# A diffusion-transformer block on one core: instructions of the attention stage kept at the program's place on their engines, and a read of a score bank moved

## The chip, the cores and the metric

The kernel runs on one core of a Trainium2 chip. The time is device time in microseconds (us) of one execution. The core has a matrix engine, TensorE (PE in the profile; its weight loads are listed as PEld), and VectorE (DVE), ScalarE (ACT), GpSimd (POOL) and SyncE (SP, which here issues transfers only). Each engine takes its instructions in the order of its own queue; semaphores order them between engines. POOL's queue issues transfers too.

## The reference

One block over 1024 tokens of width 2048, with 256 context tokens, 8 attention heads with two score maps each, pooling, convolution, and 16 experts:

```python
hx = modulate(rmsnorm(x, norm1_g), ...)          # hc the same of the context
qx, kx, vx, px, bx, cx, ix = split_groups(hx @ w_in)
k_all, v_all = concat(kc, rope(kx)), concat(vc, vx)         # 1280 keys
s = einsum('bqhmd,bkhmd->bhmqk', rope(qx), k_all) * 64 ** -0.5   # m = 0, 1
a = softmax(s)
att = einsum('bhqk,bkhe->bqhe', a[:, :, 0] - lam * a[:, :, 1], v_all)
pool = ((window sums of px) / count - px) @ pool_w * pool_scale  # windows 2, 4, 8, 16
z = cx * ix
conv = bx * (z[t - 1] * conv_w[0] + z[t] * conv_w[1] + z[t + 1] * conv_w[2])
x = x + mod * (concat(rmsnorm(att), pool, conv) @ w_out)
x = x + mod * expert_choice_ffn(modulate(rmsnorm(x, norm2_g)))   # 128 tokens an expert
return rmsnorm(x, final_g)
```

## The kernel before

The program goes through modulation and normalisation, the projections, the attention, the output projection with the normalisation and router behind it, and the experts. The change is in the attention.

**Attention steps.** There are 64 steps: one of 8 heads, one block of 256 tokens (`b`), and one half of it of 128 rows (`qt`). `score(i)` makes 18 matmuls for step i. They fill one PSUM tile `sc` of 128 x 2560 f32, which is five banks of 512 columns: columns 0 to 1279 are the first map, 1280 to 2559 the second. Each map is cut into three column groups (`CH`) that don't cross a bank, with three products for each; `PAIRED` (L920) lays both maps' products side by side, one map's on the upper 64 rows of the PE array and the other's on the lower 64. The bank of columns 1024 to 1535 holds the end of the first map, which comes first in its order, and the start of the second, which comes last in its order. Between the two stands a small read on ACT, "turned" (L965), of two columns of that bank. Then for each map DVE takes the maximum (`nm`, L970) and ACT the exponential with its sum (`e`, L975).

`combine(i)` divides the two sums (the reciprocal of L982, then L983, L984) and subtracts the second map's exponentials from the first's (L987). `turn` transposes the result on PE (`trw`), ACT casts it (`wth`, L1000) and DVE takes the rest (`wtl`, L1001). `value` multiplies by V once per two steps (`av`).

**What runs beside them.** Between these operations filler matmuls of the projections and of the output projection run on PE (`gm`); their weights are split in two parts by ACT (L439) and POOL (L440). `next_block()` (L910) is called at the start of each step: it computes the block that the previous call loaded, and loads the next one. A block is a pooling block (bias on ACT, L861; sums on POOL, L864 to L872; a matmul) or a convolution block (first product on ACT, L896; L897, L898 and L900 on DVE, in four blocks L902 on POOL in place of L900; then a split by L500 on ACT and L502 on DVE). There are 16 of each. Their data come by SP from DRAM into two buffers (`pl_x`, and `cv_z` in the same ring).

**Loads.** `load_q`, `load_k` and `load_v` issue from POOL's queue. K and Q have two buffers each. The step's part of the loop, in the program's order, is:

```python
next_block()
...
if nn and steps[nn][2] == 0:
    load_q(*steps[nn][:2])      # nn = i + 3
if new2:                        # step nn begins another head
    load_k(visit[nn])
...
even=['C', 'S', 0.3, 'V', 0.35, 0.0, 'T0', 0.3, 'T1', 'T2', 0.05],
odd=['C', 'S', 0.25, 'T0', 0.4, 'T1', 0.2, 'T2', 0.15],
```

'C' is `combine(i + 1)`, 'S' is `score(i + 2)`, 'V' `value`, 'T0' to 'T2' `turn`, and a number a share of the filler.

**What sets the order.** The program is written in that order, but `TileContext(schedule_with_timeline_sim=True)` reorders each engine's queue by a simulated timeline, within the dependencies. An instruction can so stand on its engine's queue far ahead of its place in the program, or behind it. `tc.keep_in_program_order(ins)` ties an instruction behind the one that the program issued just before it on the same engine. It adds no wait on the chip; it holds that instruction from floating ahead of that one, and no other instruction.

Of the kernel before, what the change touches and what calls it, by code (L numbers as in the profile page):

```python
# [9 lines left out]
F32 = mybir.dt.float32  # L10
# [4 lines left out]
AF = mybir.ActivationFunctionType  # L15
# [5 lines left out]
P = 128  # L21
# [6 lines left out]
QB = 256  # L28
# [128 lines left out]
def nosync(tc, later, earlier):  # L157
    if earlier is not None:
        tc.add_manual_dep(later.ins, earlier.ins.name,
                          mybir.DependencyInfo(mybir.DependencyClass.NoSync, mybir.DependencyReason.DATA),  # L160
                          reason="accumulation groups of one bank in order")


def block_kernel(tc, I, out, dbg=None):
    nc = tc.nc
    pe, act, dve, gp, sp = nc.tensor, nc.scalar, nc.vector, nc.gpsimd, nc.sync
# [3 lines left out]
    def mm(o, l, r, start=True, stop=True):  # L170
        return pe.matmul(o, l, r, start=start, stop=stop, skip_group_check=True)  # L171

    dr = mk("dram", space=DRAM)
    kS = [dr.tile([P, 2, NKEY], F32R, name=f"kS{h}") for h in range(HEADS)]
    qS = [dr.tile([P, 2, SEQ], F32R, name=f"qS{h}") for h in range(HEADS)]
    vS = [dr.tile([P, 2, NKEY], F32R, name=f"vS{h}") for h in range(HEADS)]
# [42 lines left out]
    cw_col = colB[:, 37:49]  # L219
# [9 lines left out]
    bias_pg = lsm  # L229
# [6 lines left out]
    def tr_bank(name, pool=None):  # L236
        return (pool or ptr).tile([P, 512], F32, name=name, tag="tr")
# [5 lines left out]
    t = tr_bank("trv")  # L243
# [250 lines left out]
    def hl_store(src, n, scale, dst, pool, bufs, key=None, bias=None, tag="e_hl"):  # L494
        p = pool.tile([P, 2, 512], F32R, name=tag, tag=tag, bufs=bufs)
        if bias is not None:
            act.activation(p[:, 0, :n], src, AF.Identity, bias=bias)
            dve.scalar_tensor_tensor(p[:, 1, :n], src, bias, raw(p[:, 0, :n]), op0=ALU.add, op1=ALU.subtract)
        else:
            act.activation(p[:, 0, :n], src, AF.Copy, scale=scale)  # L500
            if isinstance(scale, float) and scale == 1.0:
                dve.tensor_tensor(p[:, 1, :n], src, raw(p[:, 0, :n]), op=ALU.subtract)  # L502
            else:
                dve.scalar_tensor_tensor(p[:, 1, :n], src, scale, raw(p[:, 0, :n]), op0=ALU.mult, op1=ALU.subtract)
        step = P // len(dst)
        for i, d in enumerate(dst):
            sp.dma_start(raw(d), raw(p[i * step:(i + 1) * step, :, :n]))
        written.add(key)
# [66 lines left out]
    def run_chunk(*args, beside=None):  # L575
        c = ChunkA(*args)
        for k in range(KT):
            if beside:
                next(beside, None)
            c.step(k)  # L580
        run_later()
        return c
# [67 lines left out]
    for h in range(HEADS):  # L650
        c = run_chunk(OFF_Q + h * P)
# [7 lines left out]
    for g in range(4):  # L659
        c = run_chunk(OFF_GC + g * P)  # L660
# [4 lines left out]
        c = run_chunk(OFF_X + g * P)  # L665
# [10 lines left out]
    t = tr_bank("trm")  # L676
# [13 lines left out]
    sc = psc.tile([P, 2 * NKEY], F32, name="sc")  # L690
# [6 lines left out]
    asm = mk("asm", bufs=2, side="right")  # L697
# [69 lines left out]
    def after(n, f, kind="b"):  # L767
        due.append((pos["tick"] + n, kind, f))
        due.sort(key=lambda d: d[0])
# [88 lines left out]
        return lambda: pool_block(g, b, x, cn, biased)  # L858

    def pool_block(g, b, x, cn, biased):  # L860
        act.activation(biased, biased, AF.Identity, bias=bias_pg[:, g:g + 1])  # L861
        w = POOL_WINDOWS[g]
        y = evB.tile([P, WP], F32, name="pl_y", tag="pl_y", bufs=3)
        gp.tensor_tensor(y[:, 1:WP], x[:, 0:WP - 1], x[:, 1:WP], op=ALU.add)  # L864
        lo, hi, sh = 1, WP, 1
        while 2 * sh < w:
            y2 = evB.tile([P, WP], F32, name="pl_y", tag="pl_y", bufs=3)
            gp.tensor_tensor(y2[:, lo + sh:hi - sh], y[:, lo:hi - 2 * sh], y[:, lo + 2 * sh:hi], op=ALU.add)
            lo, hi, sh, y = lo + sh, hi - sh, 2 * sh, y2
        m = y[:, HALO:HALO + QB]  # L870
        gp.tensor_tensor(m, m, cn, op=ALU.mult)
        gp.tensor_tensor(m, m, x[:, HALO:HALO + QB], op=ALU.subtract)  # L872

        def rest():
            t = tr_bank("trp")
            mm(t[:, 0:QB], pw[:, g], m)
            hl_store(t[:, 0:QB], QB, psc_col[:, g:g + 1], [mixP[b][:, :, g, :]], evb, T["mhl"], ("m", b, g), tag="m_hl")
        after(T["a_pool"], rest)
# [14 lines left out]

    def conv_block(g, b, z, gb):
        y = evB.tile([P, QB], F32, name="e_out", tag="e_out", bufs=T["eo"])
        act.activation(y, z[:, 0:QB], AF.Copy, scale=cw_col[:, g:g + 1])  # L896
        dve.scalar_tensor_tensor(y, z[:, 1:1 + QB], cw_col[:, 4 + g:5 + g], y, op0=ALU.mult, op1=ALU.add)  # L897
        dve.scalar_tensor_tensor(y, z[:, 2:2 + QB], cw_col[:, 8 + g:9 + g], y, op0=ALU.mult, op1=ALU.add)  # L898
        if b < 3:
            dve.scalar_tensor_tensor(y, gb, bias_pg[:, 4 + g:5 + g], y, op0=ALU.add, op1=ALU.mult)  # L900
        else:
            gp.tensor_tensor(y, y, gb, op=ALU.mult)  # L902
        hl_store(y, QB, 1.0, [mixP[b][:, :, 4 + g, :]], evb, T["mhl"], ("m", b, 4 + g), tag="m_hl")
# [29 lines left out]
    K_, V_, Q_, E_, W_ = {}, {}, {}, {}, {}  # L933

    def load_k(v):
        assert ("k", v[0]) in written
        K_[v] = ksp.tile([P, 2, NKEY], F32R, name="ks", tag="ks")
        gp.dma_start(K_[v], kS[v[0]])

    def load_v(v, l):  # L940
        assert ("v", v[0]) in written
        t = vsp.tile([P, NKEY // P, P], F32R, name="vh" if l == 0 else "vl", tag=f"v{l}", bufs=2 - l)
        gp.dma_start(t, vS[v[0]][:, l].rearrange("p (k e) -> p k e", e=P))
        V_[v, l] = t

    def load_q(h, b):
        assert b < 3 or ("q", h) in written
        q = qsp.tile([P, 2, QB], F32R, name="qs", tag="qs")
        gp.dma_start(q, qS[h][:, :, b * QB:(b + 1) * QB])
        Q_[h, b] = q  # L950

    last_stt = [None]
# [2 lines left out]
    def score(i):  # L955
        h, b, qt = steps[i]
        q = Q_[h, b]
        k = K_[visit[i]]
        for _, m, c, n in PAIRED:
            c0, c1 = CH[m][c]  # L960
            rows = slice(64 * m, 64 * m + 64)
            one = mm(sc[:, m * NKEY + c0:m * NKEY + c1], q[rows, n // 2, qt * P:(qt + 1) * P], k[rows, n % 2, c0:c1],
               start=(n == 0), stop=(n == 2))
            if (m, c, n) == (0, 0, 2):
                act.copy(asm.tile([P, 2], F32, name="turned", tag="turned"), sc[:, c0:c0 + 2])  # L965
        scored.append(one)
        for m in range(2):
            s = sc[:, m * NKEY:(m + 1) * NKEY]
            nm = asm.tile([P, 1], F32, name="nm", tag=f"nm{m}")
            r = dve.tensor_reduce(nm, s, axis=AX, op=ALU.max, negate=True)  # L970
            if T["nsy"]:
                nosync(tc, r, last_stt[0])
            e = ep.tile([P, NKEY], F32, name=f"e{m}", tag=f"e{m}", bufs=(LEAD + 1, 2)[m])
            ssum = s0C[:, b, h, qt:qt + 1] if m == 0 else asm.tile([P, 1], F32, name="s1", tag="s1")
            act.activation(e, s, AF.Exp, bias=nm, scale=1.0, accum_out=ssum)  # L975
            E_[i, m] = (e, ssum)

    def combine(i):
        h, b, qt = steps[i]
        (e0, s0), (e1, s1) = E_[i, 0], E_.pop((i, 1))  # L980
        cf = asm.tile([P, 1], F32, name="cf", tag="cf")
        dve.reciprocal(cf, s1)  # L982
        dve.tensor_scalar(cf, cf, s0, neglam, op0=ALU.mult, op1=ALU.mult)  # L983
        dve.tensor_scalar(cf, cf, 2.0 ** 100, -(2.0 ** 100), op0=ALU.min, op1=ALU.max)  # L984
        for lo, hi in ((0, T["csplit"]), (T["csplit"], NKEY)):
            if hi > lo:
                last_stt[0] = dve.scalar_tensor_tensor(e0[:, lo:hi], e1[:, lo:hi], cf, e0[:, lo:hi], op0=ALU.mult, op1=ALU.add)  # L987
# [184 lines left out]
    if True:  # L1172
# [3 lines left out]
        sp.dma_start(pw, I["pool_w"][0].rearrange("g c d -> c g d"))  # L1176
        fill(T["f1"] - T["f0"])
        load_k(visit[0])
        load_q(*steps[0][:2])
        load_v(visit[0], 0)  # L1180
        load_v(visit[0], 1)
        fill(FIRST - T["f1"])
        run_all()
# [9 lines left out]
        for i in range(NS):  # L1193
            h, b, qt = steps[i]
# [12 lines left out]
            if new2:  # L1207
                load_k(visit[nn])
# [255 lines left out]
    t = pl.tile([P, 512], F32, name="trk", tag="rl", bufs=1)  # L1464
# [4 lines left out]
    t = pl.tile([P, 512], F32, name="trk2", tag="tr", bufs=2)  # L1469
# [119 lines left out]
    for stage in plan:  # L1589
        kind, e = stage[:2]  # L1590
# [17 lines left out]
        for k in range(nk):  # L1608
# [6 lines left out]
            if k == nk - 1:  # L1615
# [5 lines left out]
                else:  # L1621
                    y, hsl = y_[e], slice(half * 1024, (half + 1) * 1024)
# [40 lines left out]
```

## Time and profile before

| what | value |
|---|---|
| time, median of 3 runs | 3346.76 us (3344.51 to 3351.8) |
| time of the profiled execution | 3349.19 us |
| its span, first to last instruction | 3347.4 us |
| PE, DVE, ACT, POOL busy | 3070.2, 2258.2, 1768.6, 879.7 us |
| mean granted TensorE clock | 0.968 |
| PE busy, 870 to 1520 us (attention steps with blocks) | 554.61 of 650 us |
| PE busy, 1600 to 1860 us (late attention steps) | 252.09 of 260 us |
| PE busy, 2100 to 3347 us (experts) | 1155.79 of 1247 us |

The profiled execution is one of its own; its rows add up to its own time, and the difference of 1.79 us between time and span lies around the first and the last instruction. Rows of a timeline give the start in us, the duration in us, the engine, the line, the operation, output and inputs, and in brackets the idle time of the engine ahead of it with what ended it.

### The profile page before, as it was taken

How to read it: one execution, taken by the hardware profiler on the slowest of the kernel's cores; microseconds unless marked ns; L12 is line 12 of the kernel's file. 1: busy time of each engine (PE TensorE's matmuls, PEld its weight loads, DVE VectorE, ACT ScalarE, POOL GpSimd, SP SyncE). 2: the span in 40 equal slices, each digit the busy share in tenths (PEclk: the TensorE clock that was granted, in tenths of full speed). 3: DMA queues.
4: the chain of work that ended last, by engine and by line, in shares of the span. 5: the costliest groups of instructions: out<-in, count | busy, mean ns of one | idle time of the engine just before them, and what ended most of it. 6: DMA issues, size and time to landing. Idle time of an engine off the chain costs nothing. (4 is left out here: it accounts for less than half of the span.)

```text
span 3347.4 us, 48671 instructions
## 1 busy us (share of the span) xinstructions
PE 3070.2 (92%) x18783; PEld 2627.1 (78%) x18783; DVE 2258.2 (67%) x2744; ACT 1768.6 (53%) x2555; POOL 879.7 (26%) x581
## 2 busy tenths in 40 slices
PE   7999999999979889878999989699999999999995
PEld 4689989888868778777989878588777777777774
DVE  5235765662257766676555579788888888888877
ACT  5213322362245556554444344577766677676665
POOL 1001100010245555544667676220000000000021
PEclk9999999999989999999999999799999999999998
DMA  9965877633466555547787876899999999999998
GB/s 313 288 211 191 279 282 247 225 123 92 122 186 176 157 156 160 172 137 223 242 266 245 301 251 214 346 335 384 380 371 369 359 369 372 363 377 368 355 331 311
DMA packets 501851, 891.24 MB, mean 266 GB/s; under 512 B 24913, under 2 KB 356258, under 8 KB 490738
## 3 DMA queue, kind: packets, MB, share of 16 engines
q1 hardware_dynamic: 476960, 788.27, 67.2%
q0 software_dynamic: 24560, 99.83, 9.6%
q8 instruction: 147, 2.41, 0.3%
q14 instruction: 86, 0.70, 0.1%
q10 hardware_dynamic: 98, 0.03, 0.0%
HBM read 797.80 MB, written 90.23 MB: 265 GB/s over the span
## 5 line engine op out<-in xcount | busy, mean ns | idle before, releaser
L1443 DVE TENSOR_TENSOR es_t<-er_t,es_t 128x1024 fp32r<-128x1024 f32 x764 | 888.5, 1220 | 99.9 <-ACT es_t L1439 98.3
L1439 ACT CAST es_t<-er_t 128x1024 fp32r<-128x1024 f32 x768 | 775.8, 1052 | 181.0 <-PE gu L171 99.1
L440 POOL TENSOR_TENSOR w_split<-w_raw,w_split 128x1024 fp32r<-128x1024 f32 x208 | 547.1, 2636 | 441.3 <-ACT w_split L439 417.3
L171 PE MATMUL g_x<-hxh,w_split 128*128 128x512 f32 (+3 forms) x2560 | 592.5, 341 | 1.1 <-DVE w_split L440 1.1
L439 ACT CAST w_split<-w_raw 128x1024 fp32r<-128x1024 f32 x288 | 301.7, 1049 | 450.0 <-PE g_x L171 136.1
L171 PEld LDWEIGHTS g_x<-hxh,w_split 128*128 128x128 f32 x2560 | 396.7, 189 | 52.4 <-issue 9.9
L171 PE MATMUL gm<-w_split,mxh 128*128 128x256 f32 x2048 | 387.7, 289 | 11.3 <-DVE oy L1135 4.3
L171 PEld LDWEIGHTS gm<-w_split,mxh 128*128 128x128 f32 x2048 | 324.8, 194 | 17.6 <-issue 8.1
L171 PE MATMUL g_x<-hxl,w_split 128*128 128x256 f32 (+1 forms) x1280 | 331.6, 339 | 0.0
L171 PE MATMUL gu<-es_t,xh 128*128 128x512 f32 x1024 | 291.4, 405 | 22.5 <-DVE es_t L1443 22.5
L171 PE MATMUL dn<-es_t,hh 128*128 128x512 f32 x1024 | 300.0, 404 | 10.3 <-DVE es_t L1443 6.4
L171 PE MATMUL gm<-w_split,mxl 128*128 128x256 f32 x1024 | 293.9, 287 | 1.9 <-DMA mxl<-mixP 1.1
L171 PE MATMUL gg<-es_t,xh 128*128 128x512 f32 x1024 | 290.3, 400 | 1.1 <-ACT xh L1509 1.1
L171 PE MATMUL gm<-hbh,w_split 128*128 128x256 f32 x1280 | 272.8, 299 | 16.2 <-ACT e_raw L513 13.1
L970 DVE TENSOR_REDUCE nm<-sc 128x1 f32<-128x1280 f32 x128 | 190.6, 1489 | 130.2 <-ACT e L975 79.1
L975 ACT ACTIVATE e<-sc,nm 128x1280 f32<-128x1280 f32 x128 | 170.2, 1330 | 161.8 <-DVE nm L970 161.2
L171 PEld LDWEIGHTS gu<-es_t,xh 128*128 128x128 f32 x1024 | 195.1, 192 | 74.2 <-DVE es_t L1443 27.8
L171 PEld LDWEIGHTS dn<-es_t,hh 128*128 128x128 f32 x1024 | 189.6, 190 | 62.4 <-DVE es_t L1443 15.9
L1499 POOL DMA_INDIRECT xg<-h2S,idxT x16 | 23.2, 1448 | 818.9 <-PE tre L1507 738.1
L171 PEld LDWEIGHTS gm<-hbh,w_split 128*128 128x128 f32 x1280 | 214.4, 197 | 27.4 <-ACT e_raw L513 16.0
L171 PEld LDWEIGHTS gg<-es_t,xh 128*128 128x128 f32 x1024 | 190.7, 189 | 47.2 <-DVE es_t L1443 2.2
L171 PEld LDWEIGHTS g_x<-hxl,w_split 128*128 128x128 f32 x1280 | 198.2, 189 | 23.8 <-issue 3.3
(301 smaller groups left out, 5131.1 us busy)
## 6 DMA issues: line engine op xcount, KB each, us to landing
er_t<-in_w_gate SPq DMA_DIRECT2D x128, 1024.0 KB, 8.3
er_t<-in_w_down SPq DMA_DIRECT2D x128, 1024.0 KB, 8.8
er_t<-in_w_up SPq DMA_DIRECT2D x122, 1024.0 KB, 13.0
ada_w<-in_w_ada SPq DMA_DIRECT2D x192, 512.0 KB, 5.6
w_raw<-in_w_in SPq DMA_DIRECT2D x160, 512.0 KB, 4.7
w_raw<-in_w_out SPq DMA_DIRECT2D x128, 512.0 KB, 5.7
ks<-kS POOLq DMA_DIRECT2D x16, 1280.0 KB, 8.3
vh<-vS POOLq DMA_DIRECT2D x16, 640.0 KB, 5.5
```

The costliest lines, as they stand in the source:

```text
L171: return pe.matmul(o, l, r, start=start, stop=stop, skip_group_check=True)
L439: act.copy(s[:, 0], r)
L440: lo_eng.tensor_tensor(s[:, 1], r, raw(s[:, 0]), op=ALU.subtract)
L970: r = dve.tensor_reduce(nm, s, axis=AX, op=ALU.max, negate=True)
L975: act.activation(e, s, AF.Exp, bias=nm, scale=1.0, accum_out=ssum)
L1439: c = act.copy(s[:, 0], r)
L1443: lo = (gp if on_gp else dve).tensor_tensor(s[:, 1], r, raw(s[:, 0]), op=ALU.subtract)
L1499: ins = gp.indirect_dma_start(out=xg, out_offset=None, in_=h2S, in_offset=bass.IndirectOffsetOnAxis(ap=idxT[:, e:e + 1], axis=0))
```

## The change

Six instructions are tied to the program's place on their engine: the pooling block's bias and the convolution's first product on ACT, the loads of K, V and Q on POOL's queue, and the reciprocal that begins the combination on DVE. The read of the shared bank is issued just before the second map's first product into that bank, which is the 15th of the 18 matmuls; before, it was issued behind the first map's last product into it, the 4th.

```diff
     def pool_block(g, b, x, cn, biased):
-        act.activation(biased, biased, AF.Identity, bias=bias_pg[:, g:g + 1])
+        tc.keep_in_program_order(act.activation(biased, biased, AF.Identity, bias=bias_pg[:, g:g + 1]))
...
     def conv_block(g, b, z, gb):
         y = evB.tile([P, QB], F32, name="e_out", tag="e_out", bufs=T["eo"])
-        act.activation(y, z[:, 0:QB], AF.Copy, scale=cw_col[:, g:g + 1])
+        tc.keep_in_program_order(act.activation(y, z[:, 0:QB], AF.Copy, scale=cw_col[:, g:g + 1]))
...
-        gp.dma_start(K_[v], kS[v[0]])
+        tc.keep_in_program_order(gp.dma_start(K_[v], kS[v[0]]))
...
-        gp.dma_start(t, vS[v[0]][:, l].rearrange("p (k e) -> p k e", e=P))
+        load = gp.dma_start(t, vS[v[0]][:, l].rearrange("p (k e) -> p k e", e=P))
+        tc.keep_in_program_order(load)
...
-        gp.dma_start(q, qS[h][:, :, b * QB:(b + 1) * QB])
+        tc.keep_in_program_order(gp.dma_start(q, qS[h][:, :, b * QB:(b + 1) * QB]))
...
         for _, m, c, n in PAIRED:
             c0, c1 = CH[m][c]
             rows = slice(64 * m, 64 * m + 64)
+            if (m, c, n) == (1, 2, 0):
+                act.copy(asm.tile([P, 2], F32, name="turned", tag="turned"), sc[:, 1024:1026])
             one = mm(sc[:, m * NKEY + c0:m * NKEY + c1], q[rows, n // 2, qt * P:(qt + 1) * P], k[rows, n % 2, c0:c1],
                start=(n == 0), stop=(n == 2))
-            if (m, c, n) == (0, 0, 2):
-                act.copy(asm.tile([P, 2], F32, name="turned", tag="turned"), sc[:, c0:c0 + 2])
...
         cf = asm.tile([P, 1], F32, name="cf", tag="cf")
-        dve.reciprocal(cf, s1)
+        tc.keep_in_program_order(dve.reciprocal(cf, s1))
```

## Rows read from the trace of the kernel before

**Rows 1.** The page's head: busy time, share of the span, instructions of each engine.

```profile
PE 3070.2 (92%) x18783; PEld 2627.1 (78%) x18783; DVE 2258.2 (67%) x2744; ACT 1768.6 (53%) x2555; POOL 879.7 (26%) x581
```

**Rows 2.** Stretches: length, busy of PE, PEld, DVE, ACT, POOL, clock, DMA share, GB/s.

```profile
870.00:1520.00 650.00, 554.61 (x4101) 494.89 (x4099) 419.20 (x587) 357.65 (x725) 332.99 (x249) 0.95 0.55 163
...
1600.00:1860.00 260.00, 252.09 (x2056) 241.87 (x2057) 136.47 (x188) 126.12 (x201) 179.63 (x93) 0.99 0.79 254
```

**Rows 3.** Waits of PE, 930 to 1500 us: total, times, longest.

```profile
PE sc L171 <- ACT turned L965: 19.8, 28, 3.7
PE sc L171 <- ACT e L975: 19.8, 19, 6.7
```

**Rows 4.** Timeline of PE: first score matmuls of steps, and one score's rest.

```profile
965.39 0.62 PE L171 MATMUL sc<-ks,qs 64*128 64x256 f32 x4
...
1146.69 1.78 PE L171 MATMUL sc<-ks,qs 64*128 64x512 f32 x14 [0.26 <-ACT turned L965]
...
1246.40 0.62 PE L171 MATMUL sc<-ks,qs 64*128 64x256 f32 x4 [0.46 <-ACT e L975]
...
1336.49 0.62 PE L171 MATMUL sc<-ks,qs 64*128 64x256 f32 x4
...
1410.81 0.62 PE L171 MATMUL sc<-ks,qs 64*128 64x256 f32 x4
```

**Rows 5.** Waits of ACT, 930 to 1500 us.

```profile
ACT pl_x L861 <- DMA pl_x<-pS: 30.6, 11, 6.5
...
ACT e_out L896 <- DMA cv_z<-zS: 20.6, 6, 9.4
```

**Rows 6.** Timeline of ACT, 1394 to 1412 us: a step with two block loads.

```profile
1394.89 0.18 ACT L965 COPY turned<-sc 128x2 f32<-128x2 f32 x1
1399.27 0.51 ACT L896 ACTIVATE e_out<-cv_z,colB 128x256 f32<-128x256 f32 x1 [4.20 <-DMA cv_z<-zS]
...
1403.53 0.51 ACT L896 ACTIVATE e_out<-cv_z,colB 128x256 f32<-128x256 f32 x1 [3.56 <-DMA cv_z<-zS]
...
1411.47 0.16 ACT L965 COPY turned<-sc 128x2 f32<-128x2 f32 x1
```

**Rows 7.** DMA issues: count, KB each, median us from issue to landing.

```profile
cv_z<-zS SPq DMA_DIRECT2D x8, 129.0 KB, 4.7
```

**Rows 8.** Timelines of DVE and ACT, 1359 to 1366 us: one combination.

```profile
1359.88 0.16 DVE L982 RECIPROCAL cf<-s 128x1 f32<-128x1 f32 x1 [1.09 <-ACT e L975]
...
1360.35 0.69 DVE L1001 TENSOR_TENSOR wtl<-trw,wth 128x512 fp32r<-128x512 f32 x1
...
1361.14 1.55 DVE L987 SCALAR_TENSOR_TENSOR e<-e,cf,e 128x1280 f32<-128x1280 f32 x1
...
1364.30 1.49 DVE L970 TENSOR_REDUCE nm<-sc 128x1 f32<-128x1280 f32 x1 [0.68 <-PE sc L171]
...
1362.32 0.40 ACT L1000 CAST wth<-trw 128x256 fp32r<-128x256 f32 x1
```

**Rows 9.** Groups, 800 to 2000 us: busy, mean ns, idle ahead and its enders.

```profile
L440 POOL TENSOR_TENSOR w_split<-w_raw,w_split 128x1024 fp32r<-128x1024 f32 x187 | 495.5, 2656 | 422.5 <-ACT w_split L439 398.7 <-PE gm L171 7.9 <-PE trw L997 7.1
...
L502 DVE TENSOR_TENSOR m_hl<-e_out,m_hl 128x256 fp32r<-128x256 f32 x16 | 17.0, 1062 | 0.0
L871 POOL TENSOR_TENSOR pl_y<-pl_y,pl_c 128x256 f32<-128x256 f32 x16 | 13.9, 866 | 0.9
...
L897 DVE SCALAR_TENSOR_TENSOR e_out<-cv_z,colB,e_out 128x256 f32<-128x256 f32 x16 | 11.0, 690 | 18.4 <-ACT turned L965 9.5 <-ACT e_out L896 8.9
L900 DVE SCALAR_TENSOR_TENSOR e_out<-cv_b,lsm,e_out 128x256 f32<-128x256 f32 x12 | 10.5, 877 | 0.2
```

**Rows 10.** K: landing times, one issue on POOL, and score 24's first matmuls.

```profile
DMA to landing us min/median/max: 6.3/8.3/10.5
...
1150.32 0.57 POOL L938 DMA_DIRECT2D ks<-kS  x1
...
1230.72 1.01 PE L171 MATMUL sc<-ks,qs 64*128 64x256 f32 x4 [6.67 <-ACT e L975]
```

## Prediction

> **What bounds the kernel now.** I read the page's head first: TensorE (PE) is busy for 92% of the span, so a new order on the other engines is worth only what PE loses to them [rows 1]. The view by stretches says where that is. From 870 to 1520 us, where the attention steps and the pooling and convolution blocks run together, PE is busy for 554.61 of 650 us; from 1600 to 1860 us, the late attention steps, for 252.09 of 260 us [rows 2]. The late stage has 8 us to give in all, so the sum is made in the first stretch. What comes behind it starts when the last attention step has ended, so what the steps gain comes off the end.
>
> The waits of PE in that stretch are led by two: for the small read of the shared score bank ("turned", 19.8 us in 28 waits) and for the exponentials of the step before (19.8 us in 19 waits), which must have emptied the score tile before the next score may write it [rows 3]. So a step is a ring: score on PE, maximum on VectorE (DVE), exponential on ScalarE (ACT), the second map's maximum and exponential, and the next score. From score 3 at 965.39 to score 39 at 1410.81 are 445.42 us for 36 steps, 12.37 us each; the eight steps from 1246.40 to 1336.49, in which hardly a block runs, take 11.26 us each [rows 4]. I call that the clean step.
>
> ACT's waits show what stretches the others. ACT takes its queue in order, and it waits 30.6 us (11 times) for the data of the pooling's bias (L861) and 20.6 us (6 times) for those of the convolution's first product (L896) [rows 5]. The timeline shows one such step: the read at 1394.89, waits of 4.20 and 3.56 us for convolution data, the next read at 1411.47 [rows 6]. That step took 16.58 us.
>
> **The sum, part by part.** It is made against the profiled execution: 3349.19 us, 2.4 above the median 3346.76. 0.2% of the time, 6.7 us, is about what a measurement can tell from no change.
>
> *Pins on L861 and L896.* They add and remove no instruction. Held at their place, they run one step behind the program's place of their loads; a step lasts 11.26 us, and such a load lands 4.7 us after its issue [rows 7], so it has landed. Gone: 30.6 + 20.6 = 51.2 us of ACT time. What reaches PE is less: the step at 1394.89 waited for 7.76 us and was 16.58 - 11.26 = 5.32 us longer, a share of 0.69. Most waits are shorter than these two together and hide behind filler matmuls. I take one half, -26 us; the bounds are 0 and -51.
>
> *The read moved from behind the 4th to just before the 15th of 18 score matmuls.* Its 28 waits cost 19.8 us, of which the longest, 3.7 us, I count to the first term, since ACT comes late there from a block's load. A short one, as at 1146.69, is 0.26 us [rows 4]: the round trip with ACT free. 28 x 0.26 = 7 us of it stay if PE must wait at the new place too. The 14 matmuls behind the read take 1.78 us [rows 4]; ten of them come ahead of it now, some 1.27 us in which ACT may still be late. Left over are 19.8 - 3.7 - 7 = 9 us of a busy ACT, about half of them covered: -5 us. Bounds: 0 (the wait moves as a whole) and -16.
>
> The Trainium skill, "PSUM — Partial Sum Buffer", section "PSUM bank collisions raise a hardware error", speaks against a larger gain: different row tiles may not write one bank at the same time, and software must order them, so an order between the two maps would have to stay at the new place. By it the term is 0 and the sum 5 us higher, a rival below; the trace agrees so far as it shows the read awaited 28 times.
>
> *The clock.* It was granted at 0.95 in the first stretch and 0.99 in the late one [rows 2], of two levels, 1.2 and 2.4 GHz. The full difference, 0.04 on 555 us of matmuls, would be 22 us. Fewer long gaps give some of it back: -4 us; bounds 0 and -22.
>
> *The reciprocal kept in place (L982).* It starts the combination, whose long operation (L987, 1.55 us) must end before the maximum of the next score can run behind it. At present it floats ahead: it runs at 1359.88, a subtraction written ahead of it (L1001, 0.69 us) follows at 1360.35, and the long operation begins at 1361.14 [rows 8]. In place, all subtractions written ahead of it go first. They need ACT's cast, whose last begins at 1362.32 and takes 0.40 us; with a last subtraction of about 0.4 us and three short operations of 0.6 us together the long one begins near 1363.7 and ends at 1365.25, where the maximum began at 1364.30 [rows 8]: 0.95 us late. In the 16 steps with a convolution its four DVE operations also come first: twice 0.69, 0.88 and 1.06 us, 3.3 us in all [rows 9]. In part they lie ahead of the maximum already; a quarter of them, 0.8 us, is a value near the plain step's. Lateness counts only where the exponentials are what the next score waits for, 19 of some 46 steps [rows 3], a share of 0.4: 0.95 us x 30 plain steps x 0.4 = 11, and 0.8 x 16 x 0.4 = 5: +16 us. Bounds: 0, since DVE has slack (67% busy [rows 1]), and 16 x 3.3 = 53.
>
> *K, V and Q loads kept in place on the POOL queue (L938, L943, L949).* At present the K load of a new head runs far ahead: issued at 1150.32, used by score 24 at 1230.72, 80 us later [rows 10]. In place it is issued in the step ahead of its use, behind that step's block on POOL. K lands in 8.3 us, at most 10.5 [rows 10]. Ahead of it can stand a weight split of 2.66 us and two to six operations of 0.87 us [rows 9]: 4 to 8 us. Against a step of 11.26 us K is 8.3 + 4 - 11.26 = 1.0 to 5.0 us late where the step is short, and in time where it is long. I take four of eight heads at 1.8 us: +7 us. Bounds: 0 and 8 x 5 = 40. V is used at least a step behind its load, and Q has a fifth of K's bytes; both are taken at nothing, the step's filler matmuls being their cover; late by a step's rest they would cost as K does. POOL's own waits for a free Q buffer go too, at no gain: PE hardly waits for POOL.
>
> The Trainium skill, "DMA: Bandwidth & Descriptors", section "Anatomy of one DMA — SWDGE (gpsimd) path", fits 2.0 us and the bytes over 436e3 per us. An estimate by it for 1280 KB is 5.0 us; the row says 8.3, and the row decides. By the page K would hardly be late and the sum 7 us lower.
>
> Sum: -26 - 5 - 4 + 16 + 7 = -12 us. That is 3337 for the profiled execution and **3335 us** against the median.
>
> **The rivals.** *Every step falls to the clean length.* 36 x (12.37 - 11.26) = 40 us less, 3307 us. For it: the waited step shows 0.69 of its waits in its length. Against: the pins on the reciprocal and the loads add waits, and the clean steps did without a block's work. Chance 0.12.
>
> *Nothing that can be measured.* The block waits on ACT are hidden for the most part: PE waits for the exponentials for 19.8 us in all, so that some 13 of the first term's 26 us come off, the rest is eaten as above, and the sum is about 0: 3347 us. Chance 0.15.
>
> *The read's wait only moves.* Its term is 0 and the sum -7: 3340 us. For it: the matmuls behind the read wait although the first of them writes other columns. Against: ten matmuls more for ACT to come. Chance 0.09.
>
> *Slower by a late combination.* The convolution's four DVE operations stand ahead of the reciprocal for their full 3.3 us in all 16 steps: 53 in place of 16 makes the sum +25, 3372 us. It decides as soon as the long operation ends more than some 1.6 us behind the score's end (1364.30 less what was free ahead of it, from 1362.69). For it: DVE takes its queue in order, and the product that these operations wait for is held back too. Against: 53 needs every such step to hang on the exponentials. Chance 0.14.
>
> *Slower by late K.* Eight heads at 5 us: 40 in place of 7, sum +21, 3368 us. It decides where POOL's queue ahead of K is over 11.26 - 8.3 = 3.0 us. For it: one weight split and one operation are 3.5 us. Against: steps with a block last longer than 11.26 [rows 4]. Chance 0.10.
>
> **How the numbers follow.** The forecast keeps 0.40, with a range of its own from 3318 to 3344. The range for 8 in 10 goes from 3300, below the clean case, to 3358, some way into the slower ones. Faster by over 0.2% (below 3340): 0.37 of the forecast, 0.12 of the clean case, 0.05 of the moved wait: 0.54. Slower: 0.24 of the two last and 0.02 of the third: 0.26. Within: 0.20.
>
> **What would show it.** Right: L861 and L896 lose their DMA waits on ACT, steps of 16 us become 12 or less, PE's waits for the read shrink but stay. The reciprocal stands behind L1001 and L502 on DVE, and PE's waits for the exponentials or for DVE grow by some 16 us less what the first pins take from them. K is issued within 12 us of its use, and PE lists a few waits of 1 to 3 us for it. Wrong: waits for K at every head, or a maximum that begins 3 us behind its score's end, would make it slower; steps near 11.3 us throughout would make it much faster.

## The result, and the profile after

The changed kernel takes 3368.63 us (median of 5 runs, 3365.9 to 3369.53), the kernel before 3350.97 us beside it: ratio 1.0051, with a 95% interval of 1.0039 to 1.0063. It is slower by 18 us, where 12 us less was forecast. The profiled execution is the median one, 3368.63 us, with a span of 3366.8 us.

The head of the changed kernel's page, and its stretches as in [rows 2]:

```profile
PE 3093.3 (92%) x18783; PEld 2640.9 (78%) x18783; DVE 2295.4 (68%) x2744; ACT 1774.0 (53%) x2555; POOL 868.9 (26%) x581
```

```profile
870.00:1520.00 650.00, 560.91 (x4024) 497.54 (x4024) 422.93 (x572) 353.08 (x706) 306.79 (x237) 0.93 0.53 157
...
1600.00:1860.00 260.00, 255.66 (x2069) 242.15 (x2070) 161.49 (x204) 132.76 (x214) 177.79 (x97) 0.99 0.81 265
```

In the first stretch PE ran 4024 matmuls where it ran 4101 before [rows 2], and was busy for 6 us longer with them. Its idle time there is not longer (89.1 us of 650, before 95.4): it is slower at each matmul, with the clock granted at 0.93 against 0.95. The late stage is as full as it was.

The same holds for the whole of the two profiled executions: the same 18783 matmuls kept PE busy for 23.1 us longer [rows 1], and the rest of the span is 273.5 us, before 277.2. How much of the loss goes with the clock can't be read from one execution of each. Busy time times granted clock is 2972 us before and 2976 after, so the busy time goes with the clock; but the profiled execution before was granted 0.968, while 94 others of that kernel were granted 0.960 to 0.969, on the mean 0.9639, and the five of the changed kernel 0.9624. On 3090 us of busy PE that difference is some 5 of the 18 us, an estimate.

The waits of PE and of ACT, 930 to 1500 us, in the changed kernel (total, times, longest):

```profile
PE trw L998 <- DVE wtl L1002: 26.2, 21, 3.5
PE sc L171 <- ACT e L976: 12.1, 11, 2.9
PE sc L171 <- DMA qs<-qS: 5.2, 1, 5.2
PE sc L171 <- ACT turned L964: 5.0, 7, 1.7
```

```profile
ACT turned L964 <- PE sc L171: 66.6, 36, 4.4
```

The same view of the kernel before has one line to set beside the first:

```profile
PE trw L997 <- DVE wtl L1001: 8.9, 12, 1.8
```

Both leading waits of [rows 3] fell, from 19.8 to 5.0 and from 19.8 to 12.1 us, and the block loads of [rows 5] are gone from ACT's list. In their place PE's transposes wait for DVE's subtractions, 26.2 us against 8.9, and ACT waits for PE at the read for 66.6 us; before it stood there for 3.9 us, by the group of the read (800 to 2000 us; the columns of [rows 9]):

```profile
L965 ACT COPY turned<-sc 128x2 f32<-128x2 f32 x64 | 10.7, 167 | 4.3 <-PE sc L171 3.9
```

PE waits for no K load.

By steps (the start of the first maximum of each, from the timeline of DVE) the changed kernel is level with the one before up to step 25, which starts at 1248.1 against 1250.5. It loses 21.3 us from there to step 42: 223.6 us against 202.3. That stretch as a row of each kernel, before first:

```profile
1250.50:1452.80 202.30, 183.43 (x1420) 165.02 (x1421) 141.94 (x202) 122.62 (x255) 109.99 (x80) 0.98 0.55 164
```

```profile
1248.10:1471.70 223.60, 196.94 (x1439) 176.89 (x1437) 148.45 (x208) 125.82 (x256) 105.15 (x83) 0.92 0.50 149
```

A matmul took 196.94 / 1439 = 0.137 us on the mean, before 183.43 / 1420 = 0.129. At the old mean the 1439 would have taken 186 us. So in this pair of executions 11 of the 21.3 us come with the lower granted clock, 0.92 against 0.98, 7.8 are more idle time of PE, and 2.5 are the 19 matmuls more.

### The profile page after: what moved, and what is told of

The parts are those of the page before. It is cut to its first block, busy times and chain, and to the rows that moved or that the text cites. A ratio compares the mean times of both kernels' runs of the same rounds, so it can differ in the third digit from the quotient of the medians.

```text
span 3366.8 us, 48691 instructions
## 1 busy us (share of the span) xinstructions
PE 3093.3 (92%) x18783; PEld 2640.9 (78%) x18783; DVE 2295.4 (68%) x2744; ACT 1774.0 (53%) x2555; POOL 868.9 (26%) x581
## 3 DMA queue, kind: packets, MB, share of 16 engines
q1 hardware_dynamic: 476960, 788.27, 66.6%
## 5 line engine op out<-in xcount | busy, mean ns | idle before, releaser
L440 POOL TENSOR_TENSOR w_split<-w_raw,w_split 128x1024 fp32r<-128x1024 f32 x208 | 532.8, 2569 | 531.3 <-ACT w_split L439 506.8
L171 PE MATMUL gm<-hbh,w_split 128*128 128x256 f32 x1280 | 265.6, 298 | 8.4 <-ACT e_raw L513 7.8
```

Of the source, the lines that this page charges most:

```text
L440: lo_eng.tensor_tensor(s[:, 1], r, raw(s[:, 0]), op=ALU.subtract)
```

## The experiments

I call the parts act (pins on the bias L861 and the first product L896), rec (pin on the reciprocal), load (pins on the K, V and Q loads) and turn (the moved read). The theories' letters are their own: A and B name the reciprocal and the read as the cause, L the loads, C chance by a new order, D and E prices that add or that exist only together, P the place of the loads on POOL's queue. Each run was timed in 5 rounds against the kernel before on the same chip; 0.001 of the time is 3.4 us. The intervals are about 0.0015 to either side.

| kernel | parts | ratio, 95% interval |
|---|---|---|
| changed | act rec load turn | 1.0051 (1.0039 to 1.0063) |
| no_rec | act load turn | 0.9953 (0.9936 to 0.9971) |
| no_turn | act rec load | 1.0043 (1.0028 to 1.0057) |
| no_load | act rec turn | 0.9948 (0.9929 to 0.9966) |
| no_act | rec load turn | 1.0022 (1.0008 to 1.0035) |
| only_act | act | 0.9926 (0.9913 to 0.9939) |
| only_rec | rec | 1.0084 (1.0071 to 1.0097) |
| only_load | load | 1.0013 (1.0005 to 1.0022) |
| only_turn | turn | 1.0064 (1.0045 to 1.0084) |
| act_turn | act turn | 0.9959 (0.9942 to 0.9975) |
| act_rec | act rec | 1.0007 (0.9996 to 1.0018) |
| act_load | act load | 1.0081 (1.0063 to 1.0100) |
| rec_turn | rec turn | 1.0037 (1.0024 to 1.0049) |

**One part taken out.** Each is the changed kernel with the lines of one part as they were before.

```diff
 no_rec
-        tc.keep_in_program_order(dve.reciprocal(cf, s1))
+        dve.reciprocal(cf, s1)
```

> The change without the reciprocal's pin. Theory A (the pinned reciprocal starts the combination late, and the transposes on PE wait for what is behind it on DVE): the loss of 18 us is gone, some 3345 us or less, ratio 0.998 or below, and PE's waits of trw for wtl (26.2 us in the changed kernel, 10.3 before, 930 to 1520 us) fall to about 10. Theory B (the moved read holds ACT's queue until the 14th score matmul): still about 3365, ratio 1.004 or more, with ACT's 68.8 us of waiting for the score at the read unchanged. Theory C (no part does it; any change reorders the whole stage, and each part is worth a few us by chance): between, about 3360.

3339.87 us, 0.9953: theory A's time. But the waits do not follow it: PE still waits 29.2 us for the subtractions (930 to 1520 us, and the same from 930 to 1500), and ACT at the read as in the changed kernel:

```profile
PE trw L998 <- DVE wtl L1002: 29.2, 27, 2.5
```

```profile
ACT turned L964 <- PE sc L171: 66.1, 35, 4.9
```

So the pin is needed for the loss, and the wait that I had named for it is not its sign.

```diff
 no_turn
-            if (m, c, n) == (1, 2, 0):
-                act.copy(..., sc[:, 1024:1026])
             one = mm(...)
+            if (m, c, n) == (0, 0, 2):
+                act.copy(..., sc[:, c0:c0 + 2])
```

> The change with the read of the shared bank at its old place, behind the 4th matmul. Theory B (the read at the new place is waited for by ACT, 68.8 us in 37 waits against 3.9 before, and what stands behind it on ACT, the casts of the weights, comes late to DVE and PE): 3347 us or less, ratio 1.000 or below, and PE's waits of trw for wtl fall by 10 us or more. Theory A (the reciprocal): still slower by 15 us or more, ratio 1.004 to 1.007. Theory C: about 3360.

3368.58 us, 1.0043: theory B falls for the change as a whole.

```diff
 no_load
-        tc.keep_in_program_order(gp.dma_start(K_[v], kS[v[0]]))
+        gp.dma_start(K_[v], kS[v[0]])          # V and Q alike
```

> The change without the pins on the K, V and Q loads. By the trace of the changed kernel PE waits for these loads once, 5.2 us, so theories A and B both expect no change from it: about 3364 us, ratio 1.004. Theory L (the late loads, or weight splits held up behind V's load on POOL's queue, 17.8 us, cost the time without being named): 3350 us or less.

3335.56 us, 0.9948: theory L. Here too both waits stay (930 to 1500 us):

```profile
PE trw L997 <- DVE wtl L1001: 27.7, 27, 2.5
```

```profile
ACT turned L963 <- PE sc L171: 65.3, 36, 4.9
```

Taking out rec, turn, load or act gives back 0.0098, 0.0008, 0.0103 and 0.0029, together 0.0238, where the whole loss is 0.0051: the prices are not a sum.

```diff
 no_act
-        tc.keep_in_program_order(act.activation(biased, ...))
+        act.activation(biased, ...)            # the first product alike
```

> The change without the pins on the pooling's bias and the convolution's first product. My forecast's first term says that these pins bring 26 us: without them the time would be about 3390 us, ratio 1.012. If instead the waits that they took off ACT were hidden from PE for the most part, it is within 7 us of the changed kernel, 3360 to 3375; if the blocks' work, held a step longer, is itself what delays the transposes, it is faster, 3350 or less.

3360.17 us, 1.0022: the gain that I had forecast for these pins isn't there within the change.

**One part alone, or two.** Each is the kernel before with the named lines of the change.

```diff
 act_turn: the pins of pool_block and conv_block, the read before (1, 2, 0)
 only_rec: + tc.keep_in_program_order(dve.reciprocal(cf, s1))
 only_load: + tc.keep_in_program_order(...) around the loads of K, V, Q
 only_act: + tc.keep_in_program_order(act.activation(...)) twice
```

> Only the pins on the bias and on the first product, and the moved read; neither the reciprocal nor the loads are pinned. The changed kernel stands at ratio 1.0051, without the reciprocal's pin at 0.9953, without the loads' pins at 0.9948. Theory D (each of the two pins costs on its own, the reciprocal on DVE and the loads at the opening and on POOL): the costs add, ratio 0.985, some 3303 us. Theory E (the two do harm only together, and either one alone does none): ratio 0.995, some 3335 us. Theory C (a new order of the whole stage costs a few us by chance, whatever is pinned): anywhere within 0.995 to 1.005 with no sum.

3337.36 us, 0.9959: not the sum (0.985). Without rec and load it is where it is with one of them.

> The kernel before with the reciprocal's pin alone. Theory D: slower by its price, 0.0098, ratio 1.010, some 3385 us. Theory E: no change, ratio 0.998 to 1.002. My forecast's term for this pin was +16 us, ratio 1.005.

3382.92 us, 1.0084: close to theory D for this part, and 28 us where I had 16.

> The kernel before with the pins on the K, V and Q loads alone. Theory D: slower by its price, 0.0103, ratio 1.010. Theory E: no change, 0.998 to 1.002. My forecast's term for these pins was +7 us, ratio 1.002.

3356.86 us, 1.0013: theory E for this part; 4 us, where I had 7.

> The kernel before with the pins on the bias and the first product alone. My forecast's first term was -26 us, ratio 0.992. The changed kernel lost the 51.2 us of ACT waits for the blocks' data, and without these pins it is at 1.0022 where it is at 1.0051 with them: by that they bring nothing or cost 0.003, ratio 1.000 to 1.003. If the waits come back to PE as waits for the subtractions (wtl), ratio about 1.000 and PE's waits of trw for wtl rise from 10 to 25 us or so.

3329.97 us, 0.9926, 25 us faster; my first term, 26, was right by itself. It beats both kernels, and no other run is faster. ACT's one wait left for a block's data, and PE's leading waits:

```profile
PE sc L171 <- ACT e L975: 16.9, 15, 4.7
PE trw L997 <- DVE wtl L1001: 14.9, 15, 2.3
PE sc L171 <- ACT turned L965: 11.0, 19, 1.7
```

```profile
ACT pl_x L861 <- DMA pl_x<-pS: 7.9, 1, 7.9
```

The 51.2 us of [rows 5] are 7.9; the wait for the subtractions rises by 6 us, not by 15.

```diff
 act_rec: the pins of pool_block and conv_block, and the reciprocal's
 no_q: the changed kernel, load_q as before
 no_kv: the changed kernel, load_k and load_v as before
```

> The pins on the bias and the first product and the reciprocal's pin, without the loads' pins and with the read at its old place. Alone the first give 0.9926 and the reciprocal's 1.0084; with the moved read beside them the two give 0.9948. If the prices add, 1.001. If the moved read is what made the reciprocal's pin harmless (it lets the subtractions ahead of the reciprocal run earlier: 25.9 us of them and of their casts stood ahead of it in steps 0 to 24 with the pin alone, 2.7 with the moved read), this run is at 1.001 or above and clearly slower than 0.9948. If the pins on the block's ACT work did it, it is at 0.995 as well.

3356.34 us, 1.0007: the prices of act and rec add (0.9926 + 0.0084 = 1.0010), and turn is what makes rec harmless where load is away.

> The change with K's and V's loads pinned but not Q's. Without all three pins the ratio is 0.9948, with them 1.0051. If Q's pin is the dear one (in the changed kernel the first Q stands behind the first K and lands 9.5 us after its issue, and the first score waits 5.2 us for it; only the opening is touched, some 5 us), the gain is no more than 5 us of the 34: ratio 1.003 to 1.004, unless the steps gain as well. If K's pin is the dear one, ratio 1.004 to 1.006.

3340.69 us, 0.9965 (0.9951 to 0.9978).

> The change with Q's load pinned but not K's and V's. My forecast gave the loads 7 us, all to K: ratio 1.003. If K's and V's pins are the dear ones (V's second half stands on POOL's queue for 17.8 us behind the value matmuls, and weight splits behind it), ratio 0.996 or below. If Q's is, ratio 1.004 to 1.006.

3334.97 us, 0.9955 (0.9941 to 0.9969). Either Q's pin or K's and V's can be taken out, and all is back: neither load is the dear one.

**The place of the pinned reciprocal.** div_first is the changed kernel with the reciprocal written ahead of the block; rec_early is the kernel before with rec, written half a step earlier still.

```diff
 div_first
...
+            if i + 1 < NS:
+                divide(i + 1)        # the pinned reciprocal alone
             next_block()
...
 rec_early
...
                 elif op[0] == "T":
+                    if op == "T1" and i + 2 < NS:
+                        divide(i + 2)
                     turn(i, int(op[1]))
```

> The change with one difference: the reciprocal, still pinned, is written at the head of the step, ahead of the block, and not behind it. So the convolution's four operations on DVE no longer stand ahead of it; what the step before wrote (its last subtractions) still does. In the changed kernel the reciprocal comes 1.82 us behind the exponentials in steps 0 to 24, and 20 of these 45 us are the convolution's operations. Theory A1 (the convolution's operations ahead of the reciprocal are the loss): the delay falls under 0.8 us and the ratio to 0.995 to 0.998. Theory A2 (the subtractions, or the pin as such): delay and ratio stay, 1.003 to 1.006.

3366.48 us, 1.0045 (1.0033 to 1.0058), with the delay down from 1.82 to 1.12 us in steps 0 to 24, short of A1's 0.8: A2 in time. The convolution's operations ahead of the reciprocal are not what the change costs.

> The kernel before with the reciprocal pinned as in the change, but written half a step earlier: in the step ahead, just before the second of the three turns. So the last subtractions of that step and the block's DVE operations stand behind it on DVE and not ahead of it. Behind place alone the pin gave 1.0084, with the reciprocal 2.46 us behind the exponentials in steps 0 to 24. Theory A (what stands ahead of the reciprocal is the price): the delay falls under 0.5 us and the ratio to 0.998 to 1.002. Rival (the pin as such, or the new order of the queues that comes with any pin): 1.005 or more.

3364.2 us, 1.0036 (1.0021 to 1.0050); the delay is 1.07 us in steps 0 to 24 and 0.23 in 25 to 41. Between the two: over half of the price (0.0084 to 0.0036) goes with the place, some 12 us stay though the delay is less than half.

**The read alone and with rec, and act with load.**

```diff
 only_turn: the read before (1, 2, 0)
 rec_turn: that, and the reciprocal's pin
 act_load: the pins of pool_block and conv_block, and those of the loads
```

> The kernel before with the moved read alone. With the pins on the block's ACT work beside it the move costs 0.0033 (0.9926 to 0.9959). My forecast's term was -5 us, ratio 0.9985. If the move lengthens the way from the exponentials to the last four score matmuls in any case, 1.002 to 1.004; if it takes the waits for the read off PE (19.8 us before) and these count, 0.995 to 0.998.

3375.47 us, 1.0064: slower by 21 us, dearer than any expectation. PE and ACT, 930 to 1500 us:

```profile
PE trw L997 <- DVE wtl L1001: 37.3, 24, 4.4
...
PE sc L171 <- ACT turned L963: 15.2, 10, 4.0
```

```profile
ACT turned L963 <- PE sc L171: 51.3, 29, 5.4
```

The read is awaited by PE for 4.6 us less than in [rows 3]. But ACT now stands at it for 51.3 us until the 14th matmul is done, and the transposes wait 28.4 us more for the subtractions, which need ACT's casts.

> The reciprocal's pin and the moved read alone. If prices add: 1.0084 and that of the read alone, 1.008 to 1.012. If the moved read takes most of the reciprocal's price away, as it does with the pins on the block's ACT work beside it (1.0007 to 0.9948): 1.001 to 1.004, and the reciprocal's delay falls from 2.46 us to about 1.

3362.85 us, 1.0037; the delay is 1.04 us in steps 0 to 24. rec costs nothing beside turn (1.0064 to 1.0037).

> The pins on the block's ACT work and on the loads, without the reciprocal's pin and with the read at its old place. If the prices add (0.9926 and 1.0013): 0.994. If the loads' pins cost 33 us wherever the blocks' ACT work is in its place: 1.002 or more.

3381.03 us, 1.0081: the price of load is 0.0013 by itself and 0.0155, 52 us, beside act. Its dearest step, 28.7 us from 1144.8 to 1173.5 where the kernel before takes 15.7, accounts for 13 of them; on POOL and on PE:

```profile
1149.76 2.41 POOL L440 TENSOR_TENSOR w_split<-w_raw,w_split 128x1024 fp32r<-128x1024 f32 x1
1152.11 0.59 POOL L943 DMA_DIRECT2D vh<-vS  x1
...
1154.59 3.47 POOL L440 TENSOR_TENSOR w_split<-w_raw,w_split 128x1024 fp32r<-128x1024 f32 x1 [0.47 <-ACT w_split L439]
1158.03 0.90 POOL L872 TENSOR_TENSOR pl_y<-pl_y,pl_x 128x256 f32<-128x256 f32 x1
1158.87 0.75 POOL L950 DMA_DIRECT2D qs<-qS  x1
1159.62 0.56 POOL L938 DMA_DIRECT2D ks<-kS  x1
```

```profile
1158.98 1.22 PE L171 MATMUL trp<-pl_y,pw 128*128 128x256 f32 x2 [6.87 <-POOL pl_y L872]
...
1169.59 0.59 PE L171 MATMUL sc<-ks,qs 64*128 64x256 f32 x4 [2.68 <-DMA ks<-kS]
```

POOL takes its queue in order: the block's last sum comes behind two weight splits, PE waits 6.87 us for it at the pooling matmul, and only behind the sum are Q and K issued; 9.97 us later the score starts, having waited 2.68 us for K. The gap costs more than its length: behind it, from 1159.0 to 1164.4 us, the clock was granted at 0.51, where the lower of its two levels, 1.2 GHz, is 0.5, and the value matmuls start 0.21 us apart; from 1164.4 us, at 1.00, they start 0.12 us apart.

**The loads ahead of the block.** al_loads_first is act_load, loads_first the changed kernel; in both the loads of K and Q are written in front of the block.

```diff
+            if nn and steps[nn][2] == 0:
+                load_q(*steps[nn][:2])
+            if new2:
+                load_k(visit[nn])
             next_block()
-            (the same lines behind it)
```

> The pins on the blocks' ACT work and on the loads (1.0081 together), with the K and Q loads of a step written ahead of its block and not behind it. Theory P (the loads stand behind the block's sums on POOL, and land late: in the run of the two pins K is issued at 1159.62 behind a sum that ends at 1158.93, and the score waits; PE waits 10.2 us for K and 8.5 us for sums): the waits for K fall under 3 us and the ratio to 0.994 to 0.998. Rival (the order of PE's queue, a transpose or a pooling matmul in front of other work): 1.004 or more, with waits as before.

3337.55 us, 0.9957 (0.9940 to 0.9974): 0.0124 of the 0.0155 are back, the time of theory P. Between 930 and 1500 us, where the blocks run, PE's waits for K fell from 6.9 us to none and those for sums from 8.5 to 1.1 us. Behind 1500 us the waits for K rose from 3.3 to 8.6 us, so that over the whole run they fell from 10.2 to 8.6 us only. The loads now stand in front of a block's sums on POOL:

```profile
1125.91 0.74 POOL L950 DMA_DIRECT2D qs<-qS  x1
1126.65 0.57 POOL L938 DMA_DIRECT2D ks<-kS  x1
...
1140.78 0.63 POOL L864 TENSOR_TENSOR pl_y<-pl_x 128x271 f32<-128x271 f32 x1 [1.92 <-ACT pl_x L861]
```

> The whole change with the K and Q loads of a step written ahead of its block. Theory P: the 0.0103 that the loads' pins cost here goes, ratio 0.995 to 0.998. Rival (the order of PE's queue): 1.003 to 1.006; the value matmuls stay split over two steps from step 29 on, as in the changed kernel, where without the loads' pins they stand together.

3349.29 us, 0.9990 (0.9979 to 1.0002): 0.0061 of 0.0103. That lies between theory P and the rival; the value matmuls stay split over steps 29 and 30 as the rival says. So moving the K and Q loads ahead of the block gives back more than half of what the loads' pins cost in the change; the rest goes with the order on PE or is not told apart. An edit that moves the loads also gives the other queues a new order, and what that is worth by itself was not measured.

## Why the prediction was wrong

By themselves the four parts measure -25 (act), +28 (rec), +4 (load) and +21 us (turn), +28 together; the forecast had -26, +16, +7 and -5. The step that failed is the addition: **"Sum: -26 - 5 - 4 + 16 + 7 = -12 us"** gives each part one price against the kernel before, whatever stands beside it. The runs show no such prices. Without rec the change is at -16 us and without load at -17, with both at +18: in this company each of the two is worth about 33 us, where they were priced at 16 and 7. Two terms were mis-sized besides. The read, **"about half of them covered: -5 us"** with bounds 0 and -16, costs 21 us alone, the largest miss of the four; but it is not what turned the sign of the change, which is as slow without it (no_turn). The reciprocal alone costs 28 us in place of 16.

Most of the signs that were to show the forecast right came. The block waits left ACT's list, PE's waits for the read shrank and stayed, the reciprocal stands behind the subtractions, and PE's waits for DVE's subtractions grew by 17 us. The waits for K did not come, and step 17 still takes 15.6 us (15.7 before). The kernel is slower all the same, and no_rec and no_load, 33 us faster, have nearly the same waits. These waits don't give the time.

*act.* Right in mechanism wherever the loads are free, and near in size, though the half that I took of the 51.2 us was a choice: 0.0074 off alone, 0.0077 beside rec, 0.0105 beside turn, 0.0089 beside both. Beside load the same pins cost 0.0068 (only_load to act_load) and in the whole change 0.0029 (no_act to the changed kernel). They hold a block's sums back, and the pinned loads stand behind those on POOL; al_loads_first gives most of that price back by another place, loads_first more than half of it in the change.

*turn.* I priced PE's wait at the read and not ACT's. At the old place the read needs four matmuls, at the new one fourteen, and ACT's queue stands behind it. The Trainium skill, "PSUM — Partial Sum Buffer", section "PSUM bank collisions raise a hardware error", has software order two row tiles in a bank, and by that rule a rival of the prediction let the wait move at no gain and no loss. The trace agrees that the wait stays and moves, to 66.6 us on ACT in the changed kernel. Alone the move is a loss of 21 us, with 51.3 us of ACT's waits. That these waits are the price is not shown: no_rec and no_load have 66.1 and 65.3 us of them and are faster than the kernel before. Beside act the move costs 0.0033. Beside rec it brings 0.0047, 0.0059 beside act and rec, and 0.0128 beside act and load (act_load to no_rec); in the whole change it makes no difference (1.0043 and 1.0051). That less then stands ahead of the reciprocal fits the delays of 2.46 us in only_rec and 1.04 in rec_turn, but was not tested by itself.

*rec.* What stands ahead of the pinned reciprocal was read rightly, how long was not: over steps 0 to 24 of only_rec it starts 2.46 us behind the exponentials' sum (25 pairs from the timelines of ACT and DVE), in the kernel before 0.03; I had 0.95 and 0.8. Of these 61.5 us 14.7 are DVE waiting for ACT's casts, which I had counted for one step alone. One such place in the changed kernel, ACT first:

```profile
1397.88 0.21 ACT L976 ACTIVATION_READ_ACCUMULATOR e<-sc,nm 128x1 f32 x1
```

```profile
1395.96 2.35 DVE L502 TENSOR_TENSOR m_hl<-e_out,m_hl 128x256 fp32r<-128x256 f32 x1 [2.07 <-ACT m_hl L500]
1398.24 0.47 DVE L504 SCALAR_TENSOR_TENSOR m_hl<-trp,colB,m_hl 128x256 fp32r<-128x256 f32 x1
1398.63 0.67 DVE L1002 TENSOR_TENSOR wtl<-trw,wth 128x512 fp32r<-128x512 f32 x1
1399.23 0.14 DVE L983 RECIPROCAL cf<-s 128x1 f32<-128x1 f32 x1
```

The sum is there at 1398.09; what is left of one operation and two others of the block and the turn go first. The place carries over half of the price (rec_early), but the delay by itself does not give it: in no_load it is 1.83 us over steps 0 to 24, in the changed kernel 1.82, and no_load is at 0.9948. In steps 50 to 62 of the changed kernel the reciprocal is 7.0 us late and costs nothing that is seen: PE is busy for 255.66 of 260 us there. The rival "slower by a late combination" gave 3372 us, near the 3368.63 measured, by luck: div_first takes the convolution's operations from in front of it and keeps the time.

*load.* Alone it was small, as forecast. The rival "late K" gave 3368 us, the time measured, and that is luck too, for it named the wrong wait: in the changed kernel PE waits for no K, and K lands 8.6 us (median) after its issue, about as before.

*The clock* moved the other way, from 0.95 to 0.93 in the first stretch, where I had it give back 4 us and nothing as the bound. It is no part by itself, but a share of each part's price: only_rec was granted 0.9586 on the mean of its executions and only_act 0.9677, the kernel before 0.9639. On 3090 us of busy PE that is some 17 us of the 28 lost and 12 of the 25 gained, estimates.

*Open.* Each pin also changes the order that the framework's schedule gives to what is left free, PE's queue among it. Why rec costs 0.0098 beside act, load and turn, and nothing beside act and turn, isn't settled. Nor is why load, dear beside act and beside act, rec and turn, costs nothing beside act and turn (0.9959 and 0.9953), or which new order holds the 12 us that rec_early keeps. Theory C, that a new order is worth something by itself, stands beside every price here; it would have to reach from -43 us (turn beside act and load) to +52 us (load beside act).

## What to carry to other kernels

A wait that leaves the busy engine's list may stand on an engine that feeds it: PE's 19.8 us at a read became ACT's 66.6 us. But neither list gives the time: kernels with nearly the same waits lie 33 us apart here. Parts of such a change are to be timed alone, in pairs and each taken out: here act alone gained 25 us (only_act), and with the other three parts beside it the gain was gone. A load that is kept in place was better written in front of the compute of its step on the queue that issues it, in both kernels tried.

## What the runs showed that I had not expected

The same pins on ACT changed their sign with what was pinned on POOL: -0.0074 without the loads' pins and +0.0068 beside them, a difference of 48 us. And a delay of 6.87 us at a single pooling matmul, with the loads behind it, went with a step of 28.7 us, where the same step (17, from 1148.5) took 15.7 us before.
